# Dividing the attention output per group of four heads, with a float32r one-hot product

## The chip, the cores and the metric

The kernel runs on one core of a Trainium2 chip. A core has five engines with queues of their own: TensorE (PE), VectorE (DVE), ScalarE (ACT), GpSimd (POOL) and SyncE (SP, which issues the DMAs). The metric is the device time of one execution in microseconds (us), lower being better. The numbers of PE busy time come from matmuls whose ends are modelled, so slots (from one start to the next) are used here more than durations.

## The reference

Two encoder layers over 512 tokens of width 1024, in float32. In each layer one input projection feeds an attention group (8 query heads of width 64, 2 key/value heads, so 4 query heads share one key head) and a Mamba-2 state-space group (SSD); both results are joined, projected and added to the residual, and a SwiGLU feed-forward block follows. The part that the change touches:

```
s = einsum("bqgrd,bkgd->bgrqk", qi, k)      # scores of one 128-query block
p = softmax(s, axis=-1)                     # exp(s - max) / sum
out = einsum("bgrqk,bkgd->bqgrd", p, v)
...
mixed = concatenate([attn_out, ssd_out])    # then x + mixed @ w_out
```

The division by the sum can be made after the product with v, since the sum is one number per query and head.

## The kernel before

Large matrix products take each float32 operand as a sum of two float32r parts ("hi" and "lo") and make three float32r matmuls of them (L410 to L412, with moving tiles of 512 columns; L418 to L420 with 256). Weights come by DMA, ACT casts the hi part (L191) and DVE subtracts it to get the lo part (L192).

A layer's mixer runs three generators that are drained in turn. `fill` makes the projections (convolution inputs, q, z) and then the first half of the output projection, `out_half(1)`, which needs the SSD result alone. `ssd` makes the scan chunk by chunk (`scores`, `chunk`), and `finish` scales its rows: POOL multiplies by the gate, ACT squares and sums (L905, tile `jk`), DVE takes a reciprocal root and scales (L912), and `to_mixed` transposes the result on PE (L824) and splits it in hi and lo. `att` goes through 8 blocks, two key groups g by four query blocks c, and each block has four heads. One head: two score matmuls (L693, L694) into a bank of the tag `s`, the row maximum on DVE (L695), exp on ACT with its row sum into `sums` (L697), four transposes on PE (L700), a copy to SBUF on ACT (L91, `t_ring`), and for each pair of heads the product with v (L710), whose result ACT copies into `qr`. The tags `s`, `t`, `m` and `a` have two PSUM banks each.

When all 8 blocks are done and z is projected, `normalize` makes the division for all 8 heads. It builds a one-hot matrix `sel` of 8 rows on POOL, takes the reciprocal of `sums` (L674), transposes it so that heads lie on 8 partitions (L677), copies that to SBUF (L679), and per pair of heads spreads 1/sum over 128 partitions by a float32 matmul of 8 rows by 512 columns (L682). DVE multiplies `qr` by the result (L684), ACT casts the hi part of `mixed` (L686) and DVE subtracts for the lo part. After it `out_half(0)` makes the other half of the output projection, whose k tiles 0 to 3 are the attention's four pairs of heads.

The order of instructions on each engine is set when the program is built: a list scheduler walks the recorded instructions by program order and readiness, with its own estimates of time, and `tc.high_priority()` puts a piece ahead. At run time each engine takes its queue strictly in that order and waits by semaphores. A bank of a tag is reused in program order, so a later tile of the tag waits until the readers of the tile two before it are done.

Of the kernel before, what the change touches and what calls it, by code (L numbers as in the profile page):

```python
# [15 lines left out]
F32 = mybir.dt.float32  # L16
F32R = mybir.dt.float32r
I32 = mybir.dt.int32
AF = mybir.ActivationFunctionType
ALU = mybir.AluOpType  # L20
# [3 lines left out]
P = 128  # L24
# [3 lines left out]
S = 512  # L28
NC = S // P
# [17 lines left out]
B1, B2, B3, BR = 2, 2, 3, 2  # L47
# [22 lines left out]
def merge(a, b, c):  # L70
    return a.rearrange("p (b c) -> p b c", b=b, c=c)
# [7 lines left out]
def tile_hybrid_encoder(ctx, tc, xt_d, par_d, rope_d, snw_d, w_kvdt, w_xbc, w_q, w_z, w_out, w_gate, w_up, w_down, out_d):  # L79
    nc = tc.nc  # L80
    V, A, G, T = nc.vector, nc.scalar, nc.gpsimd, nc.tensor
# [11 lines left out]
    def tt(e, *args):  # L93
        (G if e == "G" else V).tensor_tensor(*args)  # L94

    def bank(tag):


        return psum.tile([P, S], F32, name=f"ps_{tag}", tag=tag)
# [9 lines left out]
    for l in range(L):  # L109
# [3 lines left out]
        for what in ORDER:  # L113
            i, lo = int(what[1]), what in POOL_LO
# [136 lines left out]
    ident = const.tile([P, P], F32, name="ident")  # L251
# [193 lines left out]
    def mixer(l, norm, mx):  # L445
# [21 lines left out]
        base = mx.tile([P, 2, NC, 64], F32, name="base", tag="t2", bufs=B2)  # L467
# [29 lines left out]
        if l == 0:  # L497
            for t, rows, v in ((segr, (0, 32), 1.0), (segl, (64, 72), -1.0)):
                G.memset(t.bitcast(F32), 0.0)
                for r in rows:  # L500
                    G.affine_select(out=t, in_=t.bitcast(F32), pattern=[[-1, 8], [0, P]], compare_op=ALU.not_equal, fill=v,
                                    base=-r, channel_multiplier=1)
# [142 lines left out]
        def ring(which):  # L645
            turn[which] += 1
            return rings[which][:, turn[which] % 4]
# [14 lines left out]

        sums = mx.tile([P, NC, 8], F32, name="sums")

        def normalize():


            sel = ring("p")[:8]
            G.memset(sel, 0.0)
            pick = merge(sel, 8, 64)  # L670
            G.affine_select(out=pick, in_=pick, pattern=[[-1, 8], [0, 64]], compare_op=ALU.not_equal, fill=1.0,
                            base=0, channel_multiplier=1)
            rec = mx.tile([P, NC, 8], F32, name="rec")
            V.reciprocal(rec, sums)  # L674
            tp = bank("t")
            for c in range(NC):
                T.transpose(tp[:8, c * P:(c + 1) * P], rec[:, c], ident)  # L677
            rows = ring("p")[:8]
            A.copy(rows, tp[:8])  # L679
            for j in range(4):  # L680
                b = bank("s")
                T.matmul(b, lhsT=sel[:, j * P:(j + 1) * P], rhs=rows, start=True, stop=True)  # L682
                o = qr.rearrange("p c (j a) d -> p j c (a d)", a=2)[:, j]
                V.tensor_tensor(o, o, merge(b, NC, P), ALU.mult)  # L684
                h = merge(mixed.h[j], NC, P)
                A.copy(h, o)  # L686
                tt(MLE, merge(mixed.l[j], NC, P), o, h.bitcast(F32), ALU.subtract)

        def attention(c, g, qh, ql):
            nm = mx.tile([P, 4], F32, name="nm", tag="nm", bufs=2)  # L690
            for j in range(4):
                s_ = bank("s")
                T.matmul(s_, lhsT=qh[:, j * P:(j + 1) * P], rhs=KK[:, g], start=True, stop=False)  # L693
                T.matmul(s_, lhsT=ql[:, j * P:(j + 1) * P], rhs=KK[:, g], start=False, stop=True)  # L694
                V.tensor_reduce(nm[:, j:j + 1], s_, AX.X, ALU.max, negate=True)  # L695
                p_ = ring("p")
                A.activation(p_, s_, AF.Exp, bias=nm[:, j:j + 1], accum_out=sums[:, c, 4 * g + j:4 * g + j + 1])  # L697
                t_ = bank("t")
                for kt in range(NC):
                    T.transpose(t_[:, kt * P:(kt + 1) * P], p_[:, kt * P:(kt + 1) * P], ident)  # L700
                pt = merge(ring("t"), NC, P)
                copy(PTE[j], pt, merge(t_, NC, P))
                if j % 2 == 0:
                    first = pt
                    continue
                o_ = bank(O_BANK)

                for kt in range(NC):
                    for e, t2 in enumerate((first, pt)):
                        T.matmul(o_[64 * e:64 * e + 64, :P], lhsT=Vt[:, kt, g * 64:(g + 1) * 64],  # L710
                                 rhs=t2[:, kt], start=kt == 0, stop=kt == NC - 1)
                copy(OUTE, qr[:, c, 4 * g + j - 1:4 * g + j + 1].rearrange("p h d -> p (h d)"), o_[:, :P])
                yield
# [89 lines left out]
        done = []  # L803
# [75 lines left out]
        def att():  # L879
            todo = [(c, g) for g in range(2) for c in range(NC)]  # L880
            ready = None
            for i, (c, g) in enumerate(todo):
                while g not in qri:
                    yield
                now = ready or queries(c, g)
                ready = None
                if i + 1 < len(todo) and todo[i + 1][1] in qri:
                    ready = queries(*todo[i + 1])
                yield from attention(c, g, *now)
            while "z" not in done:  # L890
                yield
            with tc.high_priority():
                normalize()
            done.append("att")

        def finish(cs):
# [63 lines left out]
    for l in range(L):  # L960
        with tc.tile_pool(name=f"mx{l}", bufs=1) as mx:
            norm = mixer(l, norm, mx)
        with tc.tile_pool(name=f"ff{l}", bufs=1) as ff:
# [113 lines left out]
            for a, b in PHASES:  # L1077
# [5 lines left out]
                for m in range(KT):  # L1083
                    ps = bank("as"[m % 2])
                    w1, w2 = W.next()
                    for cols in norm.columns(m) if final else [slice(0, S)]:
                        halves = slice(cols.start // 256, cols.stop // 256)
                        for f in range(a, b):
                            o = (f - a) * P
                            h, g = (t[:, halves] for t in hidden(f))  # L1090
# [94 lines left out]
```

## Time and profile before

| quantity | value |
|---|---|
| median of 3 runs | 1233.36 us (1232.76 to 1242.53) |
| the profiled execution's own time | 1236.18 us |
| its span, first to last instruction | 1234.4 us |
| mean granted TensorE clock | 0.987 of full speed |
| PE busy | 1204.1 us, 98% of the span |
| DVE, ACT, POOL busy | 911.0, 626.9, 169.9 us |

The profile's page gives busy times per engine, the span in 40 slices with the granted clock of TensorE, the chain of work that ended last and the costliest groups of instructions by line. The trace behind it can be asked for a timeline of one engine (start, length, line, operation, tiles, and in brackets the idle time before with what ended it) and for the busy time and granted clock in any stretch.

### The profile page before, as it was taken

The page shows a single profiled execution, that of the slowest core. Times are in us where ns is not written, and L with a number is a line of the kernel's source. Part 1 is how long each engine was busy: PE and PEld are TensorE (multiplying, and loading weights), DVE is VectorE, ACT ScalarE, POOL GpSimd, SP SyncE. Part 2 cuts the span into 40 slices and gives each one's busy share as a digit, 9 for nine tenths or more (in the row PEclk, how much of TensorE's full clock was granted, in tenths as well). Part 3 has the DMA queues.
Part 4 walks back from the last instruction along what each step waited for, and adds up shares of the span by engine and source line. Part 5 has one row for each costly group of instructions (what it writes and reads, how often), then busy time and mean ns, then how long its engine had stood idle before and what let it go on. Part 6 is the DMA issues. An engine that isn't in the chain of part 4 may idle for free.

```text
span 1234.4 us, 19748 instructions
## 1 busy us (share of the span) xinstructions
PE 1204.1 (98%) x7718; PEld 1062.9 (86%) x7718; DVE 911.0 (74%) x1475; ACT 626.9 (51%) x1197; POOL 169.9 (14%) x148
## 2 busy tenths in 40 slices
PE   7999999999999999999999999999999999999996
PEld 6889887687899899899898898776879989989985
DVE  7898886457887677677679977845698847847843
ACT  4668676344354354254555776743444533533544
POOL 5202443011100000000212144401020000000002
PEclk8999999999999999999999999998999999999998
DMA  5321112224334234231442211212243242232122
GB/s 192 104 87 55 44 35 70 69 68 132 99 121 123 65 116 128 64 104 39 134 137 90 69 35 61 87 35 68 77 145 112 95 119 95 93 119 98 35 67 79
DMA packets 47532, 110.04 MB, mean 89 GB/s; under 512 B 5424, under 2 KB 5936, under 8 KB 47440
## 3 DMA queue, kind: packets, MB, share of 16 engines
q1 hardware_dynamic: 47440, 108.79, 27.9%
q8 instruction: 60, 0.98, 0.3%
q14 instruction: 32, 0.26, 0.1%
HBM read 104.44 MB, written 4.33 MB: 88 GB/s over the span
## 4 chain that ended last, share of the span: by engine, by line
PE 83%; DVE 10%; ACT 2%; issue 2%; POOL 1%; DMA 0%; DVEq 0%; POOLq 0%; ACTq 0%
PE ps_a L1047 6%; PE ps_a L1046 6%; PE ps_a L1045 6%; PE ps_a L410 5%; PE ps_a L411 5%; PE ps_a L412 5%; PE ps_a L1092 3%; PE ps_a L1091 3%; PE ps_a L1093 3%; PE ps_s L1091 3%; PE ps_s L1092 3%; PE ps_s L1093 3%; PE ps_s L1047 3%; PE ps_s L1046 3%; PE ps_s L1045 3%; PE ps_t L710 3%
## 5 line engine op out<-in xcount | busy, mean ns | idle before, releaser
L191 ACT CAST whi<-wraw 128x512 fp32r<-128x512 f32 (+4 forms) x185 | 126.8, 713 | 225.3 <-PE ps_a L411 59.3
L191 ACT CAST whi<-sraw 128x1024 fp32r<-128x1024 f32 x126 | 131.6, 1050 | 141.0 <-DVE sraw L166 40.7
L192 DVE TENSOR_TENSOR wlo<-wraw,whi 128x512 fp32r<-128x512 f32 (+4 forms) x185 | 153.3, 840 | 56.5 <-ACT whi L191 55.3
L192 DVE TENSOR_TENSOR wlo<-sraw,whi 128x1024 fp32r<-128x1024 f32 x126 | 153.5, 1223 | 46.3 <-ACT whi L191 46.0
L410 PE MATMUL ps_a<-xh,whi 128*128 128x512 f32 x320 | 128.3, 405 | 5.4 <-DVE a__3014 L988 1.6
L412 PE MATMUL ps_a<-xh,wlo 128*128 128x512 f32 x320 | 128.3, 401 | 0.0
L411 PE MATMUL ps_a<-xl,whi 128*128 128x512 f32 x320 | 128.0, 401 | 0.0
L322 POOL TENSOR_TENSOR ssq<-ssq,sqt 128x512 f32<-128x512 f32 x17 | 24.9, 1467 | 673.9 <-ACT sqt L319 673.6
L166 DVE TENSOR_TENSOR sraw<-sraw 128x1024 f32<-128x1024 f32 x72 | 88.0, 1222 | 1.0
L418 PE MATMUL ps_a<-whi,xh 128*128 128x256 f32 (+1 forms) x256 | 75.4, 297 | 8.1 <-ACT whi L191 8.1
L1047 PE MATMUL ps_a<-ss,wlo 128*128 128x256 f32 x288 | 81.7, 284 | 0.0
L1045 PE MATMUL ps_a<-ss,whi 128*128 128x256 f32 x288 | 81.5, 283 | 0.0
L1046 PE MATMUL ps_a<-ss,whi 128*128 128x256 f32 x288 | 81.5, 283 | 0.0
L410 PEld LDWEIGHTS ps_a<-xh,whi 128*128 128x128 f32 x320 | 61.6, 193 | 23.1 <-ACT s L1006 4.0
L1047 PE MATMUL ps_a<-s,wlo 128*128 128x256 f32 x288 | 81.1, 283 | 0.0
L1046 PE MATMUL ps_a<-s,whi 128*128 128x256 f32 x288 | 81.1, 283 | 0.0
L1045 PE MATMUL ps_a<-s,whi 128*128 128x256 f32 x288 | 79.8, 283 | 0.0
L419 PE MATMUL ps_a<-wlo,xh 128*128 128x256 f32 (+1 forms) x256 | 75.1, 294 | 0.3 <-DVE wlo L192 0.2
L411 PEld LDWEIGHTS ps_a<-xl,whi 128*128 128x128 f32 x320 | 61.5, 192 | 15.6 <-DVE xl L94 1.5
L412 PEld LDWEIGHTS ps_a<-xh,wlo 128*128 128x128 f32 x320 | 61.4, 192 | 14.7 <-issue 2.0
L420 PE MATMUL ps_a<-whi,xl 128*128 128x256 f32 (+1 forms) x256 | 73.7, 290 | 0.2 <-DVE xl L307 0.2
L1091 PE MATMUL ps_s<-hid,whi 128*128 128x512 f32 (+1 forms) x182 | 69.9, 384 | 0.0
(398 smaller groups left out, 3436.7 us busy)
## 6 DMA issues: line engine op xcount, KB each, us to landing
sraw<-in_w_gate SPq DMA_DIRECT2D x72, 256.0 KB, 2.9
sraw<-in_w_up SPq DMA_DIRECT2D x72, 256.0 KB, 4.3
wraw<-in_w_down SPq DMA_DIRECT2D x48, 384.0 KB, 3.5
wraw<-in_w_xbc SPq DMA_DIRECT2D x16, 512.0 KB, 3.6
wraw<-in_w_out SPq DMA_DIRECT2D x16, 512.0 KB, 3.6
wraw<-in_w_q SPq DMA_DIRECT2D x8, 512.0 KB, 3.3
wraw<-in_w_z SPq DMA_DIRECT2D x8, 512.0 KB, 3.2
wraw<-in_w_gate SPq DMA_DIRECT2D x8, 512.0 KB, 3.3
```

The lines of the kernel that those rows point to most:

```text
L166: V.tensor_tensor(q[to], q[to], q[by], ALU.add)
L191: A.copy(hi[:, u], raw[:, u])
L192: (G if lo_pool else V).tensor_tensor(lo[:, u], raw[:, u], hi[:, u].bitcast(F32), ALU.subtract)
L410: T.matmul(ps, lhsT=wh, rhs=op.h[k], start=first, stop=False)
L411: T.matmul(ps, lhsT=wh, rhs=op.l[k], start=False, stop=False)
L412: T.matmul(ps, lhsT=wl, rhs=op.h[k], start=False, stop=last)
L418: T.matmul(ps, lhsT=xh, rhs=wh, start=first, stop=False)
L419: T.matmul(ps, lhsT=xh, rhs=wl, start=False, stop=False)
L1045: T.matmul(out, lhsT=wh[:, o:o + P], rhs=x_[:, 0, i], start=first and i + j == 0, stop=False, skip_group_check=True)
L1046: T.matmul(out, lhsT=wh[:, o:o + P], rhs=x_[:, 1, i], start=False, stop=False, skip_group_check=True)
L1047: T.matmul(out, lhsT=wl[:, o:o + P], rhs=x_[:, 0, i], start=False, stop=i == 3, skip_group_check=True)
L1091: T.matmul(ps[:, cols], lhsT=w1[:, o:o + P], rhs=h, start=f == a, stop=False)
```

## The change

`normalize` is called twice per layer, for four heads each. The call for group 0 is made in program order right after a block of group 1 once z is projected, and without high priority; the call for group 1 comes where the one call stood, with high priority. The one-hot matrix has 36 rows: 1/sum, cast to float32r, lies on rows 0 to 3, the remainder of that cast on rows 32 to 35, and one float32r matmul of 36 rows adds the two parts while it spreads them. The one-hot matrix and the parts live in one of the two buffers of the tag `raw`, the transposed rows in another, in place of the ring of exp tiles.

```diff
-        def normalize():
-            sel = ring("p")[:8]
-            G.memset(sel, 0.0)
...
-            rec = mx.tile([P, NC, 8], F32, name="rec")
-            V.reciprocal(rec, sums)
+        one = {}
+        def normalize(g):
+            if not one:
+                t = mx.tile([P, S + 4], F32R, name="one", tag="raw", bufs=BR)
+                sel = merge(t[:36, :256], 4, 64)
+                G.memset(t[:, :400].bitcast(F32), 0.0)
+                for r in (0, 32):
+                    G.affine_select(out=sel, in_=sel.bitcast(F32), pattern=[[-1, 4], [0, 64]], compare_op=ALU.not_equal,
+                                    fill=1.0, base=-r, channel_multiplier=1)
+                one["sel"], one["rec"] = t[:36, :256], merge(t[:, 256:400], NC, 36)
+            rec = one["rec"]
+            r = mx.tile([P, NC, 4], F32, name="recip", tag="recip")
+            V.reciprocal(r, sums[:, :, 4 * g:4 * g + 4])
+            V.tensor_copy(rec[:, :, :4], r)
+            V.tensor_tensor(rec[:, :, 32:], r, rec[:, :, :4].bitcast(F32), ALU.subtract)
             tp = bank("t")
             for c in range(NC):
-                T.transpose(tp[:8, c * P:(c + 1) * P], rec[:, c], ident)
-            rows = ring("p")[:8]
-            A.copy(rows, tp[:8])
-            for j in range(4):
-                b = bank("s")
-                T.matmul(b, lhsT=sel[:, j * P:(j + 1) * P], rhs=rows, start=True, stop=True)
+                T.transpose(tp[:36, c * P:(c + 1) * P], rec[:, c].bitcast(F32), ident)
+            rows = mx.tile([P, S + 4], F32R, name="rows", tag="raw", bufs=BR)[:36, :S]
+            A.copy(rows, tp[:36])
+            for i in range(2):
+                b, j = bank("s"), 2 * g + i
+                T.matmul(b, lhsT=one["sel"][:, i * P:(i + 1) * P], rhs=rows, start=True, stop=True)
...
                 yield from attention(c, g, *now)
+                if g == 1 and not one and "z" in done:
+                    normalize(0)
             while "z" not in done:
                 yield
             with tc.high_priority():
-                normalize()
+                if not one:
+                    normalize(0)
+                normalize(1)
```

In the changed program the lines from 664 on are numbered 8 or 12 higher: the scores are L701 and L702, the maximum L703, exp L705, the transposes L708, the product with v L718, the one-hot product L690, the reciprocals' transposes L685, the multiplication L692, the casts L694, the SSD transposes L832 and the squares L917.

**PE at the end of a mixer** (layer 0; `ps_a` are the accumulators of the output projection, `xh0` the attention's half of `mixed`, `xh1` the SSD's half). Before:

```order
L411 MATMUL ps_a_2714<-xl1_2253,whi_2620 128x512
L682 MATMUL ps_s_2562<-p_ring_499 128x512
L682 MATMUL ps_s_2569<-p_ring_499 128x512
L412 MATMUL ps_a_2714<-xh1_2251,wlo_2621 128x512
L410 MATMUL ps_a_2714<-xh1_2251,whi_2620 128x512
L411 MATMUL ps_a_2714<-xl1_2253,whi_2620 128x512
L412 MATMUL ps_a_2714<-xh1_2251,wlo_2621 128x512
L682 MATMUL ps_s_2574<-p_ring_499 128x512
L410 MATMUL ps_a_2736<-xh0_2565,whi_2656 128x512
L682 MATMUL ps_s_2579<-p_ring_499 128x512
L411 MATMUL ps_a_2736<-xl0_2567,whi_2656 128x512
```

With the change:

```order
L410 MATMUL ps_a_2775<-xh0_2286,whi_2674 128x512
L411 MATMUL ps_a_2775<-xl0_2288,whi_2674 128x512
L412 MATMUL ps_a_2775<-xh0_2286,wlo_2675 128x512
L708 MATMUL ps_t_2565<-ident_91,p_ring_499 128x128 x4
L718 MATMUL ps_t_2571<-t_ring_500,Vt_429 64x128
L685 MATMUL ps_t_2585<-ident_91,one_2264 36x128 x4
L718 MATMUL ps_t_2571<-t_ring_500,Vt_429 64x128 x7
L690 MATMUL ps_s_2592<-rows_2590,one_2264 128x512
L690 MATMUL ps_s_2597<-rows_2590,one_2264 128x512
L410 MATMUL ps_a_2754<-xh0_2286,whi_2674 128x512
L410 MATMUL ps_a_2775<-xh0_2286,whi_2674 128x512
L411 MATMUL ps_a_2754<-xl0_2288,whi_2674 128x512
```

The last transposes and the last product with v now stand directly ahead of the one-hot products, and the products of the output projection that do not need group 1 all stand ahead of them; behind L690 comes a matmul that needs the cast of its own result.

**PE after the last matmul of z** (L420 of `ps_a_2152`; L832 are the SSD transposes of `to_mixed`), with the change:

```order
L420 MATMUL ps_a_2152<-whi_1725,xl1_141 128x256
L718 MATMUL ps_t_2203<-t_ring_500,Vt_429 64x128 x4
L801 MATMUL ps_m_1840<-H13_1359,CT_494 128x256 x2
L718 MATMUL ps_t_2203<-t_ring_500,Vt_429 64x128 x3
L793 MATMUL ps_m_1951<-xs_496,gg_1792 128x64 x4
L793 MATMUL ps_m_1951<-xs_496,gg_1807 128x64 x4
L685 MATMUL ps_t_2276<-ident_91,one_2264 36x128 x4
L656 MATMUL ps_t_2300<-ident_91,qd_2295 128x128 x4
L801 MATMUL ps_m_1963<-H02_1351,CT_494 128x256 x2
L690 MATMUL ps_s_2283<-rows_2281,one_2264 128x512
L690 MATMUL ps_s_2290<-rows_2281,one_2264 128x512
L832 MATMUL ps_m_2246<-ident_91,xs_496 128x128 x4
```

The first call of `normalize` stands here. Between this place and the first matmul of the output projection there are 8 pairs of score matmuls in either program; before, no further ones came later, and now 4 more pairs follow inside the output projection, so 12 heads' scores come after z where 8 did.

**ACT in the same stretch** (`jk` are the squares of `finish`, `p_ring` the exp of a head). Before:

```order
L905 ACTIVATE jk_2313,ym_2311<-xs_496 128x256
L697 ACTIVATE p_ring_499,sums_501<-ps_s_2405,nm_2404 128x512
L905 ACTIVATE jk_2316,ym_2311<-xs_496 128x256
L697 ACTIVATE p_ring_499,sums_501<-ps_s_2416,nm_2404 128x512
L91 COPY qr_497<-ps_t_2301 128x128
```

With the change:

```order
L834 CAST xh1_2251<-ps_m_2246 128x4x128
L694 CAST xh0_2286<-qr_497 128x512
L834 CAST xh1_2251<-ps_m_2257 128x4x128
L694 CAST xh0_2286<-qr_497 128x512
L917 ACTIVATE jk_2350,ym_2342<-xs_496 128x256
L917 ACTIVATE jk_2353,ym_2342<-xs_496 128x256
L705 ACTIVATE p_ring_499,sums_501<-ps_s_2310,nm_2309 128x512
L705 ACTIVATE p_ring_499,sums_501<-ps_s_2321,nm_2309 128x512
```

The two exps of the first heads after z now stand behind both squares of the last SSD chunk.

## Rows read from the trace of the kernel before

**Rows 1.** The page: engines (busy, share, instructions), granted clock in 40 slices.
```profile
PE 1204.1 (98%) x7718; PEld 1062.9 (86%) x7718; DVE 911.0 (74%) x1475; ACT 626.9 (51%) x1197; POOL 169.9 (14%) x148
...
PEclk8999999999999999999999999998999999999998
```

**Rows 2.** Stretches, PE alone: stretch, length, busy (count), granted clock, DMA share, GB/s.
```profile
182.95:211.08 28.13, 25.07 (x201) 1.00 0.27 76
...
237.50:243.55 6.05, 6.05 (x14) 0.92 0.01 3
243.55:249.27 5.72, 5.72 (x15) 0.50 0.28 93
...
783.00:810.00 27.00, 24.90 (x199) 1.00 0.26 79
...
836.60:844.15 7.55, 7.55 (x15) 0.72 0.06 9
844.15:849.86 5.71, 5.71 (x14) 0.50 0.20 80
```

**Rows 3.** Timeline of PE, end of layer 0's mixer: start, length, line, tiles.
```profile
237.51 1.98 PE L682 MATMUL ps_s<-p_ring 8*128 8x512 f32 x4
...
239.76 0.39 PE L410 MATMUL ps_a<-xh,whi 128*128 128x512 f32 x1
239.99 0.39 PE L411 MATMUL ps_a<-xl,whi 128*128 128x512 f32 x1
...
243.55 0.80 PE L411 MATMUL ps_a<-xl,whi 128*128 128x512 f32 x1
```

**Rows 4.** PE: the transposes of the reciprocals and the matmul behind (timeline).
```profile
231.17 0.60 PE L677 MATMUL ps_t<-ident,rec 128*8 128x128 f32 x4
231.69 1.09 PE L710 MATMUL ps_t<-t_ring,Vt 128*64 128x128 f32 x14
```

**Rows 5.** Line 764: count, ns min/median/max, first and last start, shape.
```profile
L764 PE MATMUL ps_m<-segr,segl x32: 391/401/503, 100.3 to 779.3; 80*128 80x512 f32 x32
```

**Rows 6.** Timelines of DVE and ACT behind the first one-hot product.
```profile
238.67 0.69 DVE L684 TENSOR_TENSOR qr<-qr,ps_s 128x512 f32<-128x512 f32 x1 [2.18 <-PE ps_s L682]
239.39 0.62 ACT L686 CAST xh<-qr 128x512 fp32r<-128x512 f32 x1 [6.31 <-DVE qr L684]
```

**Rows 7.** Timelines of PE, POOL, ACT and DVE between z and the output projection.
```profile
200.41 1.09 PE L710 MATMUL ps_t<-t_ring,Vt 128*64 128x128 f32 x14 [0.96 <-ACT t_ring L91]
...
196.15 1.28 POOL L94 TENSOR_TENSOR xs<-y,t__1966 128x512 f32<-128x512 f32 x1 [1.32 <-DVE t__1966 L796]
197.51 1.44 POOL L94 TENSOR_TENSOR xs<-xs,gz 128x256 f32<-128x256 f32 x2
...
198.70 0.69 ACT L697 ACTIVATE p_ring<-ps_s,nm 128x512 f32<-128x512 f32 x1
...
199.38 0.41 ACT L905 ACTIVATE jk<-xs 128x256 f32<-128x256 f32 x1
...
198.99 0.68 DVE L695 TENSOR_REDUCE nm<-ps_s 128x1 f32<-128x512 f32 x1
```

**Rows 8.** Gaps of PE and the clock behind them: timeline rows, then stretches.
```profile
17.42 0.82 PE L418 MATMUL ps_a<-whi,xh 128*128 128x272 f32 x2 [2.96 <-ACT whi L191]
...
299.40 0.47 PE L410 MATMUL ps_a<-xh,whi 128*128 128x512 f32 x1 [1.59 <-DVE a__3014 L988]
...
17.40:24.10 6.70, 6.49 (x27) 0.50 0.46 157
...
299.40:304.00 4.60, 4.60 (x20) 1.00 0.88 233
```

**Rows 9.** Timelines of POOL and DVE: the one-hot's selection, DVE beside POOL and alone.
```profile
211.48 0.65 POOL L671 TENSOR_SCALAR_AFFINE_SELECT p_ring<-p_ring 8x512 f32<-8x512 f32 x1
...
122.34 0.97 DVE L289 TENSOR_TENSOR qri1t<-qri1t,qm 128x16 f32<-128x16 f32 x1
...
125.35 0.18 DVE L289 TENSOR_TENSOR qri1t<-qri1t,qm 128x16 f32<-128x16 f32 x1
```

More of the change, by code (lines that the diff above doesn't have):

```diff
@@ L663, in mixer @@
         sums = mx.tile([P, NC, 8], F32, name="sums")
-        def normalize():
-            sel = ring("p")[:8]
-            G.memset(sel, 0.0)
-            pick = merge(sel, 8, 64)
-            G.affine_select(out=pick, in_=pick, pattern=[[-1, 8], [0, 64]], compare_op=ALU.not_equal, fill=1.0,
-                            base=0, channel_multiplier=1)
-            rec = mx.tile([P, NC, 8], F32, name="rec")
-            V.reciprocal(rec, sums)
+        one = {}
[13 more added lines that the diff above has]
+            V.tensor_tensor(rec[:, :, 32:], r, rec[:, :, :4].bitcast(F32), ALU.subtract)
             tp = bank("t")
             for c in range(NC):
-                T.transpose(tp[:8, c * P:(c + 1) * P], rec[:, c], ident)
-            rows = ring("p")[:8]
-            A.copy(rows, tp[:8])
-            for j in range(4):
-                b = bank("s")
-                T.matmul(b, lhsT=sel[:, j * P:(j + 1) * P], rhs=rows, start=True, stop=True)
+                T.transpose(tp[:36, c * P:(c + 1) * P], rec[:, c].bitcast(F32), ident)
[4 more added lines that the diff above has]
+                T.matmul(b, lhsT=one["sel"][:, i * P:(i + 1) * P], rhs=rows, start=True, stop=True)
                 o = qr.rearrange("p c (j a) d -> p j c (a d)", a=2)[:, j]
```

## The prediction

> **What bounds the kernel now.** The page comes first: PE is busy for 98% of the span and the other engines far less [rows 1], so time is won where PE has less to do, runs at a higher clock or waits less. The granted clock over 40 slices is full nearly everywhere, with a dip in the slice that holds the end of layer 1's mixer [rows 1]. So the second view is the stretches around the code that changes. In both layers the reader sees the same picture: the clock is full until the one-hot products start, falls during them (0.92 and 0.72 as means of those stretches) and stays at 0.50, the lower of the two levels (1.2 of 2.4 GHz), for 5.7 us behind them [rows 2]. PE has no gap there. What it did before the clock fell was to run matmuls that use 8 of 128 rows: two float32 products take 1.98 us [rows 3], while a float32r matmul of the same 512 columns takes a slot of 0.23 us at full clock (239.76 to 239.99) [rows 3]. The third view is the stretch between z's last matmul and the output projection, where PE lacks filler: 28.13 us with 25.07 busy in layer 0, 27.00 with 24.90 in layer 1 [rows 2], so 3.1 and 2.1 us of idle time.
>
> **The change, part by part.** All sums are against the profiled execution, 1236.2 us.
>
> *The one-hot products.* From the first L682 until the clock is back PE needs 6.05 + 5.72 = 11.77 us in layer 0 and 7.55 + 5.71 = 13.26 us in layer 1 [rows 2]. Besides the four L682 that holds 18 float32r matmuls: 5 between the L682 (counted in the order) and 13 behind (5.72 us at about 0.43 each). At full clock 18 cost 18 x 0.23 = 4.1 us. The four products become float32r: 4 x 0.23 = 0.9, plus 0.1 for changing over. Few rows alone don't lengthen such a matmul: L764 with 80 rows has a median of 0.40 us [rows 5], like the full ones with 0.39 [rows 3]. Saved: 11.8 - 4.1 - 1.0 = 6.7 and 13.3 - 4.1 - 1.0 = 8.2 us, together 14.9. The price of 36 rows lies between 0.23 and the old 0.98 per product (up to 3.0 us more per layer); I take 0.23, since 80 rows are nearer in type.
>
> *The transposes of 1/sum* run twice per layer. One set takes 231.69 - 231.17 = 0.5 us [rows 4], so +0.5 per layer, +1.0. Together with the products: -13.9 us.
>
> *The tail for group 1.* Before, the chain from a one-hot product to the output projection lay beside the other slow products. Now everything that does not need group 1 stands ahead of L690 in PE's order, and the matmul behind it waits for its result: DVE starts 1.1 us after an L682 pair of 1 us each starts, so about 0.5 after a short one starts, multiplies 0.69, ACT casts 0.62 directly behind [rows 6], and 0.1 to reach PE: 1.9 us, of which the two L690 cover 0.5. That is 1.4 us of idle PE, and 0.2 more for DVE's lo part. Ahead of that, L685 needs a bank of the tag `t` that ACT must first empty; such a wait stands as 0.96 us in the stretch before [rows 7]; here one L718 covers part, so 0.5. Together +2.1 per layer, +4.2; from 1.5 to 3 per layer as bounds.
>
> *The stretch after z.* The first call's L690 take both banks of the tag `s`, so the scores of the next heads wait until DVE has read them. In ACT's order the first two exps now stand behind both squares of the last SSD chunk. Those wait for POOL: 1.28 + 1.44 with small gaps, then two squares of which the second counts 0.4 to 0.5, then exp 0.6, in all 4.2 us from DVE's last `t_` to the first transposes [rows 7]. PE has 1.4 us for that time (four SSD transposes and two heads' scores), so it idles 2.8 us there, with one unbroken gap of about 2.4. About 1 us of smaller waits for SSD results stays from before. So 3.7 us idle in place of 3.1 and 2.1: +0.6 and +1.6, together +2.2, uncertain by 2 us either way per layer.
>
> *POOL and DVE.* POOL's memset and two selections move from a quiet place to the filling phase, ahead of the SSD's gate products. A selection over 512 columns takes 0.65 us [rows 9], so some 1.1 us in all. A 16-column DVE operation took 0.97 us beside POOL and 0.18 alone [rows 9], so DVE can be held up by 0 to 1.1 us per layer. DVE's own extra, four small operations and two shorter reciprocals, is under 1 us per layer. I take nothing on the path, since PE works through that phase without gaps from other matmuls; if that cover is gone it is 1.1 per layer, and this goes into the range. The Trainium skill, SBUF — State Buffer, section "SBUF: two separate sides", speaks against moving POOL work there: the port pair of DVE and GpSimd is an exclusive lock, and a DVE operation with two SBUF inputs is blocked only by a GpSimd operation that reads SBUF. The rows above agree that DVE stands for the length of a POOL operation. By the page the memset would not hold DVE up but the selections would, which as an estimate from their row is 0.7 us per layer, and the sum would be 1.4 us higher.
>
> Without a fall of the clock this is -13.9 + 4.2 + 2.2 = **-7.5 us**.
>
> *The clock.* The gap of 2.4 us stands in a stretch in which PE has little to do: between L690 and the gap come eight SSD transposes and two heads' scores, with waits of their own. Two gaps of the trace bracket it: behind one of 1.59 us the clock stayed at 1.00, behind one of 2.96 it was at 0.50 for the next 6.7 us [rows 8]. So the gap can make the clock fall, about as likely as not in each layer. A fall costs half of 6.7 = 3.3 us less the half microsecond of waits that the slower matmuls cover: 3.0, or 4.5 with a longer spell. I expect it in one of the two layers: -7.5 + 3.0 = **-4.5 us**, so 1231.7 us by the profiled execution. That execution stood 2.8 us above the median of the runs (1236.18 to 1233.36), so as a median I forecast **1229 us**.
>
> **Rivals**, given as medians in the same way.
>
> 1. *The clock never falls.* If PE's gaps come out shorter than worked out, -7.5 holds, 1226 us, and with stretches 2 us better per layer 1222. For: the falls of before inside the mixers came with the products that go. Against: the gap of 2.4 us follows from two POOL operations and an ACT order that I see.
> 2. *It falls in both layers, or at the tail instead.* The tail also has little in it: 36-column transposes, 36-row products and 1.4 us of idle. Two falls: -1.5, so 1232 us. A fall at the old place would mean that the change does not remove what it aims at.
> 3. *The heads after z become the bound (slower).* Twelve heads' scores come after z where eight did. If the four more are a serial chain through maximum (0.68) and exp (0.68 until the next operation) [rows 7] with nothing beside them, each layer pays 4 x 1.36 = 5.4 us more: -7.5 + 10.9 = +3.4, 1237 us, and with a fall per layer +9.4, 1243 us. It decides from 3.75 us per layer on, where the gain is eaten up. For: `s` has two banks and the call holds both. Against: out of the four, all scores lie inside the output projection, whose 96 matmuls of 0.23 us can cover them.
> 4. *One of the 36-row products costs like before* (0.98): +6, 1232 us without a fall. Rows of 80 speak against it.
>
> **How the numbers follow.** Chances: forecast 0.40 (1226 to 1232 with its own uncertainty), rival 1 0.22, rival 2 0.18, rival 3 0.14, rival 4 0.03, others 0.03. A difference of 1% (12 us) is about what a measurement of this kernel tells from no change. Faster by more than 1% needs 1221, beyond rival 1's better end: 0.09. Slower by more than 1% needs 1246, beyond rival 3's worse end: 0.06. Within 1%: 0.85. The range of 8 in 10 goes from 1222, rival 1's better end, to 1238, just past rival 3 without falls; the hold-up of DVE by POOL lies inside.
>
> **What would show it.** Products: L690 at about 0.4 us each with slots of 0.23. Clock: full through the output projection's start, unlike 0.50 before. Tail: a gap of some 1.4 us ahead of the first L410 behind L690, ended by ACT's cast. Stretch after z: a gap of some 2.4 us ahead of L708, ended by an exp, with the granted clock telling rivals 1 and 2 apart; from z's last matmul to the first L410 it should be shorter than the 28.1 and 27.0 us of before, since four heads have moved behind it. The prediction is wrong if the gaps sum to over 10 us per layer, if L690 runs in several passes, or if the output projection itself shows gaps at score matmuls.

## The result, and the profile after

The changed kernel takes 1242.5 us as a median (1241.0 to 1245.2) against 1233.2 us before; the ratio is 1.0066 with a 95% interval of 1.0047 to 1.0084, so it is slower, by 9 us from median to median and by 8 by the ratio. The forecast was 1229 us, with a range from 1222 to 1238. The profiled execution took 1242.39 us with a span of 1240.6 us, 6.2 us longer than the profiled execution before.

The page of the changed kernel, engines and granted clock, answering to [rows 1]:

```profile
PE 1197.1 (96%) x7718; PEld 1060.1 (85%) x7718; DVE 919.5 (74%) x1485; ACT 630.6 (51%) x1199; POOL 171.6 (14%) x150
...
PEclk9999998999999999999999999999999999999998
```

PE is busy 7.0 us less than before and yet the kernel is longer: some 13 us of new idle time. The dip of the clock has left the end of layer 1's mixer and now shows in the seventh slice, in layer 0's stretch after z.

Stretches of PE in the changed kernel (stretch, length, busy and count, granted clock, DMA share, GB/s): first the filling phase of each layer, then z to the output projection with the part at the low clock, answering to [rows 2]. The two long stretches start 1.2 us ahead of z's last matmul, so their idle time can be compared with [rows 2] but not their length:

```profile
125.20:166.45 41.25, 39.14 (x290) 1.00 0.13 40
729.40:771.20 41.80, 40.67 (x298) 1.00 0.16 51
...
184.40:212.65 28.25, 22.93 (x145) 0.82 0.22 75
197.00:207.00 10.00, 8.16 (x37) 0.50 0.13 47
...
789.00:815.55 26.55, 21.04 (x145) 0.94 0.23 81
801.50:804.50 3.00, 2.62 (x8) 0.50 0.47 175
```

After z PE idles 5.3 and 5.5 us where it idled 3.1 and 2.1, and in both layers the clock falls there. The timeline of PE in layer 0 shows where (start, length, line, tiles, in brackets the idle time before and what ended it):

```profile
191.79 0.73 PE L690 MATMUL ps_s<-rows,one 36*128 36x512 f32 x2
195.47 0.66 PE L832 MATMUL ps_m<-ident,xs 128*128 128x128 f32 x4 [2.95 <-DVE y L796]
196.67 0.88 PE L832 MATMUL ps_m<-ident,xs 128*128 128x128 f32 x4 [0.54 <-DVE t__1966 L804]
197.26 0.80 PE L701 MATMUL ps_s<-KK,qh 128*128 128x512 f32 x1
...
201.17 1.11 PE L708 MATMUL ps_t<-ident,p_ring 128*128 128x128 f32 x4 [1.83 <-ACT p_ring L705]
```

Behind the two one-hot products nothing in PE's queue can run: the SSD transposes (L832) need a bank that DVE's `y` frees, and the next heads' scores (L701) need the banks of `s` that the products hold. DVE's timeline in the same microseconds:

```profile
190.59 3.62 DVE L924 SCALAR_TENSOR_TENSOR xs<-xs,yri,snw 128x256 f32<-128x256 f32 x4
194.14 0.68 DVE L192 TENSOR_TENSOR wlo<-wraw,whi 128x512 fp32r<-128x512 f32 x1
194.74 0.67 DVE L796 TENSOR_TENSOR y<-y,ps_m 128x512 f32<-128x512 f32 x1
...
196.53 1.27 DVE L692 TENSOR_TENSOR qr<-qr,ps_s 128x512 f32<-128x512 f32 x2
```

DVE comes to `y` only after 3.6 us of scaling and a weight split, and to the reading of the products (L692) after two more operations (`ql` and `t__1966`); the first of the two banks of `s` is held from 191.8 to 197.2. Then the first exp is waited for, 1.83 us. The tail of layer 0, answering to [rows 3, 6]:

```profile
249.38 0.61 PE L685 MATMUL ps_t<-ident,one 128*36 128x128 f32 x4 [0.65 <-ACT t_ring L91]
249.93 1.09 PE L718 MATMUL ps_t<-t_ring,Vt 128*64 128x128 f32 x14
250.95 0.73 PE L690 MATMUL ps_s<-rows,one 36*128 36x512 f32 x2
252.87 0.73 PE L410 MATMUL ps_a<-xh,whi 128*128 128x512 f32 x2 [1.20 <-ACT xh L694]
```

And the filling phase of layer 0, DVE, POOL and the matmul of PE that waited, answering to [rows 9]:

```profile
121.37 4.35 DVE L284 TENSOR_SCALAR qri1i<-qm 128x16 int32<-128x16 int32 x1
```
```profile
121.26 0.41 POOL L675 TENSOR_SCALAR_AFFINE_SELECT one<-one 36x256 fp32r<-36x256 f32 x1
121.65 1.03 POOL L94 TENSOR_TENSOR xw__1331<-xs,wst 128x512 f32<-128x512 f32 x1
...
123.65 2.03 POOL L94 TENSOR_TENSOR y<-xs,par 128x512 f32<-128x512 f32 x2
```
```profile
127.80 0.47 PE L772 MATMUL ps_m<-segr,segl 80*128 80x512 f32 x1 [1.20 <-DVE qri L290]
```

L284 works on 16 columns and took 0.17 us before. Now the selection starts 0.1 us ahead of it, four products follow it on POOL without a break, and L284 ends when the last of them ends. The 1.20 us of PE are at the end of the chain that L284 begins. Layer 1 has a gap of 1.13 us in the same phase, but for another reason:

```profile
757.60 1.25 DVE L682 TENSOR_TENSOR one<-recip,one 128x16 fp32r<-128x16 f32 x1
758.77 0.68 DVE L660 TENSOR_TENSOR ql<-ps_t,qh 128x512 fp32r<-128x512 f32 x1
```
```profile
759.50 0.66 PE L708 MATMUL ps_t<-ident,p_ring 128*128 128x128 f32 x4 [1.13 <-DVE ql L660]
```

L682 is the early call's own subtraction for the second part. It works on 16 columns, took 1.25 us while a POOL product ran (757.43 to 758.82), and stands ahead of `ql`, which PE waits for. The selections come 26 us earlier there and L284 takes 0.26 us.

To weigh the terms, each layer is cut at the same four places: first score matmul, z's last matmul, first matmul of the output projection, first feed-forward matmul that waits (L410 behind `a__`). The table sums PE's idle time in these stretches (layer 0 / layer 1), from the stretches view of each run; experiments stand below.

| kernel | whole, us | idle up to z's end | idle z to projection | idle in projection | busy |
|---|---|---|---|---|---|
| before | 212.06 / 214.94 | 0.91 / 0.00 | 3.06 / 2.10 | 1.91 / 1.91 | 206.18 / 210.93 |
| changed | 216.19 / 216.65 | 2.11 / 1.13 | 5.33 / 5.51 | 3.77 / 3.48 | 204.98 / 206.53 |
| product alone (e1) | 207.82 / 210.08 | 0.85 / 0.00 | 3.06 / 2.93 | 3.33 / 3.33 | 200.58 / 203.82 |
| other banks (e7) | 206.47 / 209.25 | 2.09 / 1.13 | 2.01 / 2.04 | 1.92 / 1.92 | 200.45 / 204.16 |
| high priority (e9) | 211.29 / 214.66 | 2.10 / 0.04 | 2.92 / 2.28 | 3.17 / 3.15 | 203.10 / 209.19 |
| banks and DVE (e11) | 205.15 / 207.41 | 0.91 / 0.00 | 2.02 / 2.24 | 1.92 / 1.92 | 200.30 / 203.25 |

### The profile page after: what moved, and what is told of

Its sections match the earlier page's. It is cut to its first block, busy times and chain, and to the rows that moved or that the text cites. A ratio compares the mean times of both kernels' runs of the same rounds, so it can differ in the third digit from the quotient of the medians.

```text
span 1240.6 us, 19762 instructions
## 1 busy us (share of the span) xinstructions
PE 1197.1 (96%) x7718; PEld 1060.1 (85%) x7718; DVE 919.5 (74%) x1485; ACT 630.6 (51%) x1199; POOL 171.6 (14%) x150
## 4 chain that ended last, share of the span: by engine, by line
PE 82%; DVE 11%; issue 2%; ACT 2%; POOL 2%; DMA 0%; DVEq 0%; ACTq 0%; POOLq 0%
PE ps_a L1059 6%; PE ps_a L1058 6%; PE ps_a L1057 6%; PE ps_a L410 5%; PE ps_a L411 5%; PE ps_a L412 5%; PE ps_a L1103 3%; PE ps_a L1104 3%; PE ps_a L1105 3%; PE ps_s L1103 3%; PE ps_s L1104 3%; PE ps_s L1105 3%; PE ps_t L718 3%; PE ps_s L1059 3%; PE ps_s L1058 3%; PE ps_s L1057 3%
## 5 line engine op out<-in xcount | busy, mean ns | idle before, releaser
L192 DVE TENSOR_TENSOR wlo<-sraw,whi 128x1024 fp32r<-128x1024 f32 x126 | 153.5, 1222 | 46.5 <-ACT whi L191 46.0
L410 PE MATMUL ps_a<-xh,whi 128*128 128x512 f32 x320 | 125.8, 396 | 7.9 <-ACT xh L694 2.4
L410 PEld LDWEIGHTS ps_a<-xh,whi 128*128 128x128 f32 x320 | 60.0, 188 | 23.3 <-ACT s L1018 4.0
L420 PE MATMUL ps_a<-whi,xl 128*128 128x256 f32 (+1 forms) x256 | 74.0, 291 | 0.4 <-DVE xl L307 0.4
L412 PEld LDWEIGHTS ps_a<-xh,wlo 128*128 128x128 f32 x320 | 60.1, 188 | 12.7 <-issue 0.5
```

Source lines behind the costliest of these rows:

```text
L192: (G if lo_pool else V).tensor_tensor(lo[:, u], raw[:, u], hi[:, u].bitcast(F32), ALU.subtract)
L410: T.matmul(ps, lhsT=wh, rhs=op.h[k], start=first, stop=False)
L412: T.matmul(ps, lhsT=wl, rhs=op.h[k], start=False, stop=last)
```

## The experiments

Three batches of four, each run with the kernel before on the same chip (medians 1234.1, 1233.5 and 1233.5 us). Line numbers of an experiment differ by a few from the changed kernel's.

**e1, the product alone.** On the kernel before:

```diff
-            sel = ring("p")[:8]
+            sel = mx.tile([P, S], F32R, name="one", tag="qh", bufs=2)[:40]
...
-            V.reciprocal(rec, sums)
+            V.reciprocal(r, sums)
+            V.tensor_copy(rec[:, :, :8], r)
+            V.tensor_tensor(rec[:, :, 32:], r, rec[:, :, :8].bitcast(F32), ALU.subtract)
...
```

> The kernel before with one thing changed: the one call for all 8 heads stays where it stood, but 1/sum goes as a float32r part and its remainder on rows 0 to 7 and 32 to 39, and the four one-hot products become float32r with 40 rows. No early call, no division into groups. Theory A (the product's term of the prediction was right, and the early call of group 0 with what it makes idle ate it up): both layers lose the slow products and the half clock behind them, 6.7 + 8.2 us, less about 1 us for the longer chain ahead of the first product; 1220 us against 1233, granted clock full from the products on. Rival B (the products save little: 40 rows as two parts cost like before, or the clock falls at that place anyway because PE has little to do there): 1230 to 1234 us, granted clock again near 0.5 behind the products.

Measured 1229.2 us, ratio 0.9942 (0.9914 to 0.997). The end of layer 0's mixer, first in PE's timeline, then as a stretch:

```profile
237.76 0.73 PE L687 MATMUL ps_s<-rows,one 40*128 40x512 f32 x2
...
241.59 0.50 PE L411 MATMUL ps_a<-xl,whi 128*128 128x512 f32 x1 [0.67 <-DVE xl L94]
...
243.99 0.50 PE L411 MATMUL ps_a<-xl,whi 128*128 128x512 f32 x1 [0.75 <-DVE xl L94]
```
```profile
237.76:249.00 11.24, 9.49 (x36) 1.00 0.14 49
```

The clock stays full in the profiled execution (1227.7 us), so rival B's reason is out for it, though its range from 1230 us on is nearer to the time. Theory A's 1220 was too low: PE's busy time falls by 5.6 and 7.1 us, 12.7 together and not 14.9, and the chain from product to lo part brings two waits of 0.7 us per layer, 2.8 us where 1 was allowed.

**e2, groups with the float32 product.** The changed kernel with `t` and `rows` in F32, 4 rows, one selection and no second part.

> The changed kernel with the float32 product back (4 rows, no second part), the call per group of four heads kept where the change put it. Theory A: the early call keeps all its costs (idle in the fill, after z and at the tail, half clock after z), and the two float32 products of the tail bring about 1.3 us more per layer than the float32r pair and a half clock at the end of the mixer of about 3 us per layer: 1248 to 1253 us. Rival B (the float32r product gains nothing): the same as the changed kernel, 1241 to 1244 us.

Measured 1242.8 us, ratio 1.0055: the changed kernel's time, as rival B said, but not for its reason. The two slow products of group 0 stand in the gap after z (it shrinks from 2.95 to 1.69 us); with one selection instead of two, and no subtraction for a second part, the waits in the fill did not occur (idle up to z's end 1.07 and 0.00 us); the tail pays 0.50 of the clock for some 3 us. Without the 2.2 us less in the fill this run would be slower, so where the change put it the float32r product is worth some 2 us, against 12.7 us of busy time in e1. Over both layers this run has 8.0 us more busy time than the changed kernel, and 6.7 us less idle time after z and in the projection: most of what the product shortens was filling gaps.

**e3, both calls late.**

```diff
-                if g == 1 and not one and "z" in done:
-                    normalize(0)
```

> The changed kernel without the early call: both groups are divided at the end of the attention with high priority, still four heads each with float32r products of 36 rows, and the selection on POOL still lies in the fill. Theory A (the early call makes the gap of 2.95 us after z, the half clock behind it and the heads moved back): the stretch after z is as before, 2 to 3 us idle and the clock full; saved against before 14.9 on the products, paid 1.0 for transposes, 2.3 for the hold-up in the fill and 1 to 3 for the chain at the end: 1223 to 1226 us. Rival C (the gap and the slow clock come from having two calls or from the selections on POOL, not from the early place): the gap of about 3 us after z stays, 1235 to 1242 us.

Measured 1232.0 us, ratio 0.9976 (0.9955 to 0.9998), between the two. The gap after z is as before (3.06 us idle in layer 0), so rival C is out; the hold-up in the fill of layer 0 and the waits for lo parts stay (idle 2.11 and 3.33 us there; in layer 1, where no early call's subtraction stands ahead of `ql`, the fill idles 0.05 us), and the profiled execution has a fall of the clock from 191.5 to 194.5 us that A did not have. It comes behind a gap that the kernel before has too, where the clock stayed full [rows 2]. The matmul behind the gap, before and then in e3, with e3's stretch:

```profile
190.06 1.13 PE L793 MATMUL ps_m<-H,CT 128*128 128x256 f32 x4 [1.39 <-DVE y L788]
```
```profile
191.25 1.92 PE L801 MATMUL ps_m<-H,CT 128*128 128x256 f32 x4 [1.39 <-DVE y L796]
...
191.50:194.50 3.00, 3.00 (x12) 0.50 0.72 204
```

**e4 and e5, the gap filled.** In e4 each product of group 0 is made seven times; in e5 twice, with six full matmuls between:

```diff
...
+                for _ in range(0 if g else 6):
+                    T.matmul(b, lhsT=KK[:, 0, :P], rhs=KK[:, 1], start=True, stop=True)
...
```

> The changed kernel with each one-hot product of group 0 made seven times over (the same result written again), so that some 2.8 us of matmuls stand in the gap of 2.95 us after z and in nothing else that is waited for. Theory A (the clock falls because PE is idle there; 5.0 us in layer 0 and 2.2 us in layer 1 are lost by it): the gap shrinks to under 1 us, the clock stays full in that stretch, 1234 to 1237 us against 1242 of the changed kernel. Rival D (the clock falls for another reason, such as the 36-row products or the transposes, or the filler only moves the wait): the clock is at 0.50 behind it all the same, 1241 to 1245 us.

> The changed kernel with each one-hot product of group 0 made twice and six float32r matmuls of 128 rows by 512 columns (keys against keys, overwritten) between the two, so that the gap of 2.95 us after z is filled like in the run with seven products of 36 rows, but mostly with matmuls that use all rows. In that run the gap was gone and the clock fell to 0.50 for 10 us in layer 0 all the same. Theory F (idle time and matmuls of few rows both let the clock fall, matmuls of all rows hold it): clock 1.00 through the stretch, the 5.0 and 2.2 us of the slow clock saved, 1 to 2 us paid for the filler, 1236 to 1239 us. Rival D (the clock falls there whatever PE runs in the gap, as the waits of the following microseconds are enough): half clock again, 1245 to 1249 us, as with 36 rows.

Measured 1247.0 and 1247.7 us. In e4 (timeline, then stretches) the gap is gone:

```profile
191.96 4.00 PE L691 MATMUL ps_s<-rows,one 36*128 36x512 f32 x14
195.89 2.08 PE L833 MATMUL ps_m<-ident,xs 128*128 128x128 f32 x8
```
```profile
191.96:194.80 2.84, 2.84 (x13) 1.00 0.16 62
195.00:205.00 10.00, 8.03 (x26) 0.50 0.23 80
```

PE had no idle time and the clock fell all the same, while it ran matmuls that use 36 of 128 rows. In e5 the same place holds full matmuls:

```profile
192.08 1.65 PE L692 MATMUL ps_s<-KK 128*128 128x512 f32 x6
...
202.26 0.86 PE L712 MATMUL ps_t<-ident,p_ring 128*128 128x128 f32 x4 [2.41 <-ACT p_ring L709]
```
```profile
188.00:202.00 14.00, 10.63 (x56) 1.00 0.33 114
202.50:205.50 3.00, 3.00 (x12) 0.51 0.02 5
...
807.00:813.00 6.00, 4.32 (x15) 0.50 0.01 1
```

The clock holds through the filled place and falls behind the next gaps, in layer 0 behind 2.41 us for an exp, in layer 1 for longer than in the changed kernel. So theory F is right for the filled place alone and wrong on the time: PE now waits for the reading of the products (1.22 us) and for the exp (2.41), and the filler itself is paid. It also moves the end of the products from 192.5 to 196.4 us, and so what waits for them. What a full clock alone would be worth in this stretch is therefore not shown by either run.

**e6, the one-hot matrix from DVE.**

```diff
-                G.memset(t[:, :400].bitcast(F32), 0.0)
-                for r in (0, 32):
-                    G.affine_select(out=sel, in_=sel.bitcast(F32), pattern=[[-1, 4], [0, 64]], compare_op=ALU.not_equal,
-                                    fill=1.0, base=-r, channel_multiplier=1)
+                V.memset(t[:, 256:400].bitcast(F32), 0.0)
+                V.tensor_tensor(sel, bc(ident[:36, :4], [36, 4, 64], 2), bc(ident[:36, 32:36], [36, 4, 64], 2), ALU.add)
```

> The changed kernel with the one-hot matrix made by one DVE addition of two pieces of the identity and a DVE memset of the parts' columns, so that POOL's memset and two selections are gone; everything else stands where it stood. Theory G (POOL's selection at the start of its run of products in the fill made DVE wait 4.35 us and cost PE 1.2 us per layer): 2 to 2.5 us less than the changed kernel, 1240 us, and PE's idle time in the fill is back at 0.9 and 0.0 us. Rival H (DVE is held up there by POOL's products anyway, or the DVE operations that take their place cost as much): 1242 to 1243 us.

Measured 1241.1 us. L284 is back at 0.17 us and PE's idle time up to z's end at 0.90 and 0.00, the numbers of theory G. Its reason holds for layer 0; in layer 1 the edit takes the gap away by another order, in which the early call's subtraction (0.73 us here) and `ql` come more than 2 us earlier:

```profile
121.24 0.17 DVE L284 TENSOR_SCALAR qri1i<-qm 128x16 int32<-128x16 int32 x1
```
```profile
125.20:166.45 41.25, 40.35 (x302) 1.00 0.13 40
```

Only 1.4 us of the 2.3 reach the median, within the scatter of both kernels. In the profiled execution (1242.3 us) the clock also falls at both tails. e11 repeats the edit where no fall in the mixers disturbs it.

**e7, group 0's products in other banks.**

```diff
-                b, j = bank("s"), 2 * g + i
+                b, j = bank("s" if g else "a"), 2 * g + i
```

> The changed kernel with group 0's two one-hot products in banks of the tag a, which z has just left, in place of the tag s; group 1 as before. In the order four heads' scores now stand again ahead of z's end, and no head is held up by the early call. Theory J (the stretch after z is slow because the products of group 0 hold both banks of s, so that PE has nothing to run beside DVE's queue): idle there falls from 5.3 and 5.5 us to about 3, the clock stays full, 1233 to 1236 us with the fill's 2.3 us still paid. Rival K (it is DVE's and ACT's extra work of the early call that PE waits for, whatever the banks): 1240 to 1243 us.

Measured 1225.4 us (1225.3 to 1227.1), ratio 0.9932 (0.9913 to 0.9951): 17 us less than the changed kernel by one tag. The tag changes the scheduled order too: the score matmuls of 24 of a layer's 32 heads stand ahead of z's last matmul, as in the kernel before; in the changed kernel it is 20. The timeline and the stretches after z:

```profile
191.11 0.73 PE L690 MATMUL ps_a<-rows,one 36*128 36x512 f32 x2 [0.23 <-ACT rows L687]
191.77 0.66 PE L708 MATMUL ps_t<-ident,p_ring 128*128 128x128 f32 x4
192.18 0.70 PE L701 MATMUL ps_s<-KK,qh 128*128 128x512 f32 x2
193.28 1.13 PE L801 MATMUL ps_m<-H,CT 128*128 128x256 f32 x4 [0.40 <-DVE y L796]
```
```profile
186.10:214.00 27.90, 25.89 (x205) 1.00 0.23 76
786.00:814.00 28.00, 26.14 (x184) 1.00 0.20 58
```

Heads are in the pipeline while DVE works, and the 2.95 us for `y` are 0.40. The clock is full, and the idle time of the tail is gone too (1.92 us in the projection, as before): behind group 1's products (240.89 us in layer 0) ten matmuls of the projection run without a wait (241.54 to 243.98), and the first cast is done in that time (242.82). Theory J's reason held, and the time is 8 us better than its range. Rival K is out.

**e8, the call after the SSD**, with e6's edit: `"ssd" in done` in place of `"z" in done`.

> The changed kernel with the early call moved: group 0 is divided once the SSD is done and not once z is projected, and the one-hot matrix made by DVE as in the run without POOL's selections. In the order group 0's products then stand behind the last scan products and one head pair moves. Theory A (float32r products are worth 5.6 us per layer as measured with the product alone; what cost more was the place of the early call): no half clock behind z, 11 us saved on the products less 1.0 for transposes and 1 to 2 for the tail, 1224 to 1227 us. Rival K (an early call costs its DVE and ACT work on the path at any place ahead of the output projection): 1231 to 1236 us.

Measured 1237.1 us (1232.2 to 1242.4), ratio 1.0017. Neither theory has it, though rival K's range ends only 1 us below: behind a wait of 2.36 us for `y` the profiled execution runs at 0.50 from 191.5 to 201.0, and the products still hold both banks of `s` (waits of 0.5 us ahead of two scores), again at 0.50 from 208.5 to 214. A later place did not cure the call. How much of this is the banks, how much the moved pair of heads and how much DVE's work was not taken apart.

**e9, the early call with high priority.**

```diff
-                    normalize(0)
+                    with tc.high_priority():
+                        normalize(0)
```

> The changed kernel with the early call of group 0 under high priority; banks, matmuls and everything else as in the change. Theory L (the heads behind the call are held up because tiles of s are given out in program order, and the call itself cannot come earlier since its transposes stand in line for a bank of t behind the products of the heads before it; its rank does not matter): the next heads' scores still come behind z and the stretch still has 5 us idle with a slow clock, 1239 to 1244 us. Rival M (the call only ranks too low against z's matmuls): with the rank raised the stall goes, 1226 to 1232 us, as with other banks.

Measured 1236.2 us (1233.3 to 1239.2), ratio 1.001: half way, so both theories are partly right. In the order the four heads still stand behind z, as theory L has it, but the products stand 3 us earlier, and DVE frees the banks in time:

```profile
188.82 0.73 PE L690 MATMUL ps_s<-rows,one 36*128 36x512 f32 x2
...
193.73 0.50 PE L701 MATMUL ps_s<-KK,qh 128*128 128x512 f32 x1
...
195.52 0.66 PE L832 MATMUL ps_m<-ident,xs 128*128 128x128 f32 x4 [0.48 <-DVE y L796]
```

The gap of 2.95 us goes, and the idle time after z falls to 2.9 and 2.3 us. What separates this run from e7 is some 5 us per layer: 1.2 us of tail in each layer, and 2.7 and 5.0 us of busy time, in layer 1 with two falls of the clock. That the moved heads make it is argued: the banks of group 0's products differ as well.

**e10, e7 with the float32 product** (e2's edit on e7).

> The version with group 0's products in banks of a (1225.4 us), with the float32 product of 4 rows back for both groups. A pair of float32 products takes 1.98 us and a float32r pair 0.73. Theory N (where no gap lies beside it, the float32r product is worth its length and the clock): 2 x 2 x 1.25 = 5.0 us for the lengths, and behind group 1's pair the clock falls as it did before, about 3 us per layer: 1233 to 1237 us, granted clock 0.50 behind the pair. Rival O (two slow products in a row are too few for the clock to fall): lengths alone, 1229 to 1231 us.

Measured 1231.9 us (1229.6 to 1237.4), against 1225.4 for e7. Like e2 it has one selection and no hold-up in the fill (0.99 and 0.00 us), so the fair neighbour is e11 with 1222.7: the float32r product is worth 9 us here. Theory N's clock is seen, and behind the first pair too, in a profiled execution of 1236.6 us; the median lies between the ranges of N and O:

```profile
193.50:203.00 9.50, 9.50 (x36) 0.50 0.22 76
248.50:251.50 3.00, 3.00 (x9) 0.50 0.06 7
```

**e11, e7 with e6's edit.**

> The version with group 0's products in banks of a (1225.4 us), with the one-hot matrix made by DVE in place of POOL's memset and selections. Theory G (the selection holds DVE up in the fill, 1.2 us of PE idle per layer, and this adds to the other gain): 1.9 and 1.1 us of idle time in the fill go, 1222.5 to 1224 us. Rival H (what is won there is lost again behind, because DVE's two operations and another order take it): 1225 to 1226 us.

Measured 1222.7 us (1222.3 to 1223.3), ratio 0.9894 (0.9868 to 0.9921): faster than both kernels. Theory G's size held, 2.7 us, with the reason of layer 1 as under e6.

**e12, e1 with the lo part on POOL** (`MLE` from V to G).

> The version with the float32r product alone (one call at the end, 1229.2 us), with the subtraction for the lo part of the attention's half moved from DVE to POOL. With the product alone PE waits four times 0.7 us for DVE's lo parts. Theory P (DVE's queue makes the lo parts late: two multiplications, subtractions and weight splits in a row): the waits go, 1226 to 1227.5 us. Rival Q (POOL needs 1.3 us for what DVE does in 0.7, so the same matmuls wait longer): 1229 to 1232 us.

Measured 1228.5 us against 1229.2 for e1, within the intervals of both. The profile shows the waits gone (2.13 us idle in the projection of each layer in place of 3.33), which is theory P's mechanism; its size does not stand out in the time.

## Why the prediction was wrong

Forecast were 4.5 us less than the profiled execution before; measured are 6.2 us more. By the prediction's own steps, in us, both layers together:

| step | forecast | measured | from |
|---|---|---|---|
| one-hot products with the clock behind them | -14.9 | -12.7 | busy time, e1 against before |
| transposes | +1.0 | +1.0 | per layer 0.55 us from L685 to L718 at the tail and 0.43 after z, less 0.5 for the one set before |
| tail | +4.2 | +3.4 | idle in the projection, 3.77 and 3.48 against 1.91 |
| stretch after z | +2.2 | +5.7 | idle z to projection |
| POOL and DVE | 0 | +2.3 | idle up to z's end |
| fall of the clock | +3.0 | +5.4 | half of 8.16 and of 2.62 us of busy time at 0.50 |

They sum to +5.1 where -4.5 was forecast; the layers grew by 4.1 and 1.7 us, so 0.7 us is unassigned. Of the 9.6 us between forecast and measured, the stretch after z makes 3.5, the clock that falls in it 2.4, POOL and DVE 2.3 and the products 2.2; the tail was 0.8 better.

- **The step that failed is "The stretch after z".** It saw that the products hold both banks of `s`, and it counted twelve heads behind z instead of eight, but it gave the hold no wait of its own, as if DVE came to the products at once, and put the one long gap (2.4 us) ahead of the exps. The runs have the long gap ahead of that, 2.95 us for `y`, and then 1.83 and 1.69 us for the exp. In DVE's queue the multiplication stands behind four scalings, a weight split, `y`, `ql` and `t__1966`: 4.0 us pass from the end of the products to L692. And with the four heads moved, PE's queue held nothing that did not need DVE. e7 shows that the choice of banks makes it, at run time and through the order together: the same call in banks of `a` takes 17 us less, of which 10 are idle time and 7 busy time in the table. e9 parts the two in some measure: with the heads still moved, earlier products and a shorter hold take 2.4 and 3.2 us off the idle time after z.
- **The clock** followed from it. "One fall in one of two layers" became a fall in both, of 10 and some 3.5 us. The gap was longer than the forecast's 2.4, and on the side of the prediction's bracket where the clock fell (2.96 us with a fall, 1.59 without [rows 8]; here 2.95 with one). But the length of the gap alone does not decide: e3 has a fall behind 1.39 us, and the kernel before has none behind the same gap.
- **POOL and DVE** was taken as nothing, with 1.1 us per layer as its price if the cover was gone. It was gone: 1.2 and 1.1 us, and e6 and e11 show that both go with POOL's one-hot matrix. In layer 0 the selection that L284 stood behind makes it; in layer 1 it is the early call's own subtraction ahead of `ql`, one of the four small DVE operations that the prediction held to be off the path. Of the Trainium skill's rule (SBUF — State Buffer, "SBUF: two separate sides") the exclusive lock agrees with L284's 4.35 us in that DVE stood while POOL worked. The prediction had priced the selections by their own length, 0.7 us per layer, and not by the run of POOL products that the selection was joined to.
- **The products** were right in kind (0.73 us a pair, no falls of the clock behind them in e1, e7 and e11) and 2.2 us too high. A pair takes 0.65 us until the next matmul starts and that one 0.34 where 0.23 is usual (e7: 240.89, 241.54, 241.88 us), 0.25 more per pair than forecast and 1.0 in all; the rest was not taken apart.
- **The tail** came as told: in layer 0 1.20 us of idle time ended by ACT's cast where 1.4 was forecast, and 0.65 for L685's bank where 0.5 was.
- **Rival 3** had the moved heads, but as a chain inside the output projection. The projection showed no gap at a score matmul (of layer 0's 3.77 us idle, 1.91 were there before and 1.20 and 0.65 are the tail's); the price was paid ahead of it. That this rival's 1243 us, with a fall per layer, meets the measured 1242.5 is luck.

## What to carry to other kernels

A piece of work that is put early into a pipeline takes its place in every ring it draws from. Where it takes all buffers of a ring that later stages need, those stages stand behind it and behind whatever its reader is queued behind; a bank of another ring can be worth more than the faster instruction, here 17 us (the changed kernel against e7) against 9 (e10 against e11). Price such a hold by where the freeing instruction stands in its engine's queue, not by how long it takes. And look at what an off-path operation joins: a short one that closed the gap ahead of a run of others on POOL held up a DVE operation for the length of the run, 4.35 us.

## What the runs showed of the hardware that was not expected

- A DVE operation on 16 columns stood 4.35 us while five POOL operations ran back to back, although DVE's two-input operations on the same columns came in after one POOL operation each, 0.97 us [rows 9]. The one that stood has one input; the same line took 0.17 us where POOL's run began a little later (before, and e6). The kind of operation does not decide it alone: in layer 1 of the changed kernel the same line took 0.26 us (at 730.37) and the next one, also with one input, 0.96 us (at 730.66), while POOL's memset, two products and the selections ran without a break (729.17 to 732.48). What decides it is open.
- The granted clock fell from 1.00 to 0.50 while PE had no idle time at all, in e4 during matmuls of 36 rows and in e10 behind two float32 products of 4 rows, and held with full matmuls in the same place (e5, layer 0). Four 40-row products among full ones left it at 1.00 (e1).
- Falls came at a place in one profiled execution and not in another with the same gap: the tail of the changed kernel has none, and behind the same 1.2 us the tails of e4, e5 and e6 have 3 us at 0.50. Times of one kernel go with it: in e8 the runs of 1232 us have a mean granted clock of 0.99 and those of 1242 us 0.982, while e11, whose profile has no fall in the mixers, stays within 1222.3 to 1223.3 us at 0.993 to 0.995.
